# Routing on rows without norm factor and shift, in a two-layer mixture-of-experts kernel

## The chip, the cores and the metric

The kernel runs on one core of one Trainium2 chip. Its time is the device time of that core in microseconds, median of three runs. A core has five engines with an instruction stream each: TensorE (PE in the profile; PEld is its weight load), VectorE (DVE), ScalarE (ACT), GpSimd (POOL) and SyncE (SP), which issues most DMAs. ACT and POOL issue DMAs too. An engine executes in program order; semaphores order the engines among each other.

## The reference

A model of two layers on 256 latent and 256 context tokens of width 1024, float32. Each layer runs a mixer (attention in layer 0, an S5 scan with a gated linear unit, GLU, in layer 1) and then a mixture of 32 experts (MoE), two per token. Layer 1 computes latent tokens alone. Cut to what matters here:

```python
def rmsnorm(h, g):      return h * lax.rsqrt(jnp.mean(h * h, -1, keepdims=True) + 1e-6) * g
def modulate(h, shift, scale):  return h * (1.0 + scale) + shift
# per layer i; m_l = split of silu(c) @ mod_w[i] + mod_b[i] into 6 vectors
h = h + m_l[2] * mixer(modulate(rmsnorm(h, norm1_g[i]), m_l[0], m_l[1]))
t = modulate(rmsnorm(h, norm2_g[i]), m_l[3], m_l[4])      # rows of the MoE
g_logits = t @ w_group + b_group                           # 4 groups, best one taken
e_logits = t @ w_router + b_router                         # 32 experts, two best of the group
# combine[token, expert]: softmax weights of the two
y = sum_e combine[:, e] * ((silu(t @ w_gate[e]) * (t @ w_up[e])) @ w_down[e])
h = h + m_l[5] * y
```

Context tokens go the same way in layer 0 with vectors of their own. Per row, t = r · (h · scale) + shift, where r is the norm's factor (one number a row), and scale = (1 + m[4]) · g and shift = m[3] are vectors over the 1024 columns.

## The kernel before

All instructions are issued in a program order written by hand: generators yield between steps, and `along(main, others)` (L213) runs one step of each other generator after each step of the main one.

**Layer 0.** `attention` ends with the output products: `out(t)` (L439) for the tiles t = 0 to 3 (128 rows each; 0 and 1 context, 2 and 3 latent) issues 16 products (L445), one a round. Beside it run `beside` (products with `mod_w` for layer 1's vectors, L142, in half vectors of four steps, one half every four rounds; the last two halves run after tile 3) and, for each tile whose output is done, `Moe.prep` (L597) and `Moe.route` (L647), one step a round. After tile 3, `build` loads two experts' weights (`ahead(2)`, SP's queue) and runs what is left of the preparation, with the last `mod_w` steps between its steps. Weights pass through a pool of 1 MiB slots ("ring" and "more").

`prep(n, j)` of tile n with vectors j: row t = h · scale on VectorE (L609) and the sum of squares on ACT; r on POOL; then t = t · r + shift in two halves (L618, VectorE); in layer 0 a store of t to `td` in DRAM; eight transposes by TensorE (L626) copied into tT; logits by eight products with the router table `wr` (L632; 40 columns: 4 groups, 4 empty, 32 experts), plus the bias `br`. In layer 1 the rows are then split in a high and a low part (ACT L640, POOL L642), as transposed weights for the gather by products.

`route`: maxima, indices and one-hots on VectorE (`oh`, `ob` L673); products that count earlier tokens of each expert (L683), giving a position to each token; two one-hots "A" of the slot (L717) and products that place token numbers, later the weights, into 64 slots per expert (`place`, L719). The last tile's route calls `count` (the number of rounds of 64 slots, read at the end only).

In layer 0 `start()` (L770) then makes indices and issues three gathers on POOL's queue (L836, rows of `td` by index, 128 rows for a pair of experts), then expert 2's weights on the same queue; `turned` (L850) transposes a gathered pair. `experts` (L952) runs experts 0 to 31: `hidden` (L863) gate and up products, `down` (L884), `combine` (L928).

**Layer 1.** `s5.glu(1, wg)` is the GLU's last half: 32 steps n = 0 to 31, three products each (L1745), its weights split in high and low parts by VectorE and POOL (L1714). Between steps `build` runs two steps of tile 0's prep at n = 12, two of tile 1's at n = 16, and one of tile 0's at each even n from 18 on. The GLU's result for a tile leaves through VectorE and ACT (L1753 to L1758). What is left follows behind the GLU in the order of the string LAST, 0 and 1 being tiles and 2 `moe.opening`. `open()` (L780) makes the first four experts' rows by products of the high and low parts with one-hots of the slots (`take` L767); `quad` does it for later fours.

`load_rows` issues on POOL's queue the norm gain and the shift and scale rows, broadcast to 128 partitions (`mod.row`); `scale_rows` makes scale of them (L593); `tables` then loads `wr` (L555, L556), `br` and iotas. The end of layer 0's row loads, the tables and the output stage lie close together in time.

Of the kernel before, what the change touches and what calls it, by code (L numbers as in the profile page):

```python
# [244 lines left out]
def attention(c, mod, par, tail):  # L245
# [3 lines left out]
    with ExitStack() as ctx:  # L249
# [264 lines left out]
class Moe:  # L514
# [7 lines left out]
    def __init__(self, c, layer, tiles, wk, ps, lent=None):  # L522
# [18 lines left out]
        self.oh = wk.tile([128, nt, 2, 32], F32, name="oh")  # L541
# [25 lines left out]
    def more(self, wk, ps):  # L567

        self.wk2, self.ps2 = wk, ps
        self.opening, self.opened = self.open(), 0  # L570
        self.gates()
# [6 lines left out]
    def load_rows(self):  # L578
# [4 lines left out]
        for j in dict.fromkeys(j for _, j in self.tiles_j):  # L583
# [3 lines left out]
            self.rows[j] = r  # L587

# [7 lines left out]

    def prep(self, n, j):  # L597

# [17 lines left out]
        for f in range(2):  # L616
            s = slice(512 * f, 512 * f + 512)
            nc.vector.scalar_tensor_tensor(t[:, s], t[:, s], st[:, 3:4], shift[:, s], op0=OP.mult, op1=OP.add)  # L618
            yield
        if self.xg is not None:  # L620
            nc.scalar.dma_start(self.td[128 * n:128 * n + 128], t)
        tT = wk.tile([128, KT, 128], F32, name="tT", tag="t4", bufs=T4)
        for b in range(2):
            p = self.bank(("xt", "gu")[b])
            for k in range(4):
                nc.tensor.transpose(p[:, 128 * k:128 * k + 128], t[:, 512 * b + 128 * k:512 * b + 128 * k + 128], c.ident)  # L626
            c.evac(tT[:, 4 * b:4 * b + 4, :], p.rearrange("p (k n) -> p k n", k=4))
            yield
        yield
        p = self.bank("gu")  # L630
# [16 lines left out]
    def route(self, n, L):  # L647
# [49 lines left out]
        if self.one:  # L697
            yield
# [1262 lines left out]
```

## Time and profile before

| | |
|---|---|
| median of three runs | 1160.03 us (1157.13 to 1165.32) |
| the profiled execution | 1162.29 us, its span 1160.3 us |
| granted TensorE clock, mean | 0.951 of full speed |
| busy: TensorE / VectorE / ACT / POOL | 993.9 (86%) / 729.3 (63%) / 322.9 (28%) / 140.6 (12%) us |
| DMA | 331.75 MB, mean 286 GB/s |
| layer 0: output stage with tiles 0 to 2 / to the first expert | 283 to 383.42 / to 410.60 us |
| layer 1: GLU's last quarter / to the first expert / experts to the end | 829.60 to 859.90 / to 886.04 / to 1160.30 us |

Times of single instructions count from the span's start. A line of the timeline has the start, the busy time of a run of like instructions, engine, line of the code, output and input, their number and, in brackets, the idle time ahead and what ended it. In a table of windows "(x9)" is a number of instructions, "PEclk" the granted clock as a share of full speed (1.00 is 2.4 GHz, 0.50 is 1.2 GHz), and "DMA share" the mean busy share of 16 DMA engines.

### The profile page before, as it was taken

Reading aid. Unit: us, or ns where it says so; the run is one execution under the profiler, and the core shown is the slowest. Engines: PE = TensorE matmul, PEld = TensorE weight load, DVE = VectorE, ACT = ScalarE, POOL = GpSimd, SP = SyncE. Lnnn points to the kernel's source line nnn. Section 1 sums busy time; section 2 is a strip of 40 time slices with the busy share of each in tenths; the row PEclk is TensorE's granted clock in tenths of the full one; section 3 lists DMA queues with packets and bytes.
Section 4 is the critical chain, followed back from the end, with each engine's and each line's share of the span. In section 5 each row is a group of like instructions: output and inputs, shape, how many; then the busy total and the mean of one; then the engine's idle time right before and its main releaser. Section 6 shows DMA issues by size and latency. Waiting matters only on the chain. (4 is left out here: it accounts for less than half of the span.)

```text
span 1160.3 us, 17551 instructions
## 1 busy us (share of the span) xinstructions
PE 993.9 (86%) x6639; PEld 561.9 (48%) x6639; DVE 729.3 (63%) x1800; ACT 322.9 (28%) x703; POOL 140.6 (12%) x212
## 2 busy tenths in 40 slices
PE   2798889979998499999988876579868999999996
PEld 1443444544444355555544432365656555555552
DVE  7679988894325513555788987499874444444444
ACT  3332334343000123121221212793532212221110
POOL 2211121123100200000000002112321000000000
PEclk9999999989988789999998988889988999999998
DMA  9954854764993799999885854899976999999941
GB/s 297 340 158 149 285 211 156 263 210 166 385 342 126 274 415 415 400 410 349 326 340 214 330 209 153 201 210 316 397 264 267 378 384 378 376 379 380 382 168 37
DMA packets 88232, 331.75 MB, mean 286 GB/s; under 512 B 10040, under 2 KB 18968, under 8 KB 69712
## 3 DMA queue, kind: packets, MB, share of 16 engines
q1 hardware_dynamic: 68736, 290.05, 68.0%
q10 hardware_dynamic: 11424, 21.12, 5.2%
q0 software_dynamic: 7984, 19.42, 5.0%
q8 instruction: 54, 0.88, 0.3%
q14 instruction: 34, 0.28, 0.1%
HBM read 313.76 MB, written 20.99 MB: 289 GB/s over the span
## 5 line engine op out<-in xcount | busy, mean ns | idle before, releaser
L863 PE MATMUL gu<-ring,xq 128*64 128x256 f32 x1056 | 144.3, 388 | 2.7 <-DVE sl L868 2.6
L863 PE MATMUL gu<-more,xq 128*64 128x256 f32 x992 | 136.0, 386 | 0.8 <-DVE sl L868 0.8
L928 PE MATMUL co<-yh,oT 128*128 128x512 f32 x188 | 88.0, 468 | 26.6 <-DVE z L919 8.9
L863 PEld LDWEIGHTS gu<-ring,xq 128*64 128x64 f32 x1056 | 81.3, 139 | 60.2 <-issue 23.9
L863 PEld LDWEIGHTS gu<-more,xq 128*64 128x64 f32 x992 | 76.9, 138 | 54.4 <-issue 22.9
L352 PE MATMUL acc<-ring,uT 128*128 128x512 f32 x192 | 93.0, 617 | 2.9 <-ACT uT L328 2.9
L867 ACT ACTIVATE sl<-gu 64x256 f32<-64x256 f32 x64 | 24.1, 377 | 243.6 <-PE gu L863 243.6
L936 DVE TENSOR_TENSOR sum<-sum,co 128x512 f32<-128x512 f32 x92 | 59.5, 682 | 33.3 <-PE co L928 33.3
L928 PE MATMUL co<-yl,oT 128*128 128x512 f32 x188 | 78.2, 416 | 0.3 <-DVE yl L913 0.3
L876 DVE COPY hT<-ht 128x128 f32<-128x128 f32 x64 | 18.4, 287 | 87.0 <-PE ht L874 86.8
L868 DVE TENSOR_TENSOR sl<-gu,sl 64x256 f32<-64x256 f32 x64 | 27.3, 426 | 64.5 <-ACT sl L867 49.7
L884 PE MATMUL y<-ring,hT 128*64 128x512 f32 x272 | 67.2, 616 | 0.4 <-DVE hT L876 0.4
L928 PEld LDWEIGHTS co<-yh,oT 128*128 128x128 f32 x188 | 36.0, 191 | 61.7 <-DVE z L919 15.9
L884 PE MATMUL y<-more,hT 128*64 128x512 f32 x240 | 58.0, 604 | 0.4 <-DVE hT L876 0.4
L352 PEld LDWEIGHTS acc<-ring,uT 128*128 128x128 f32 x192 | 35.0, 196 | 37.3 <-issue 32.8
L142 PE MATMUL gv<-ring,cT 128*32 128x256 f32 x512 | 35.6, 421 | 18.2 <-DMA ring<-mod_w 18.2
L930 DVE TENSOR_TENSOR h<-h,co 128x512 f32<-128x512 f32 x64 | 41.1, 681 | 8.5 <-PE co L928 8.5
L928 PEld LDWEIGHTS co<-yl,oT 128*128 128x128 f32 x188 | 36.6, 195 | 7.5 <-DVE yl L913 4.4
L836 POOL DMA_INDIRECT xg<-td,row x16 | 16.1, 1006 | 196.6 <-PE xt L850 186.1
L407 ACT ACTIVATE pr<-sc,mx 128x256 f32<-128x256 f32 (+1 forms) x32 | 18.6, 580 | 74.7 <-DVE mx L406 74.6
L913 DVE SCALAR_TENSOR_TENSOR yl<-z,pt,yh 128x512 fp32r<-128x512 f32 x30 | 22.5, 751 | 25.4 <-ACT yh L912 25.4
L912 ACT ACTIVATE yh<-z,pt 128x512 fp32r<-128x512 f32 x30 | 21.6, 722 | 55.9 <-DVE z L919 55.9
(430 smaller groups left out, 1868.4 us busy)
## 6 DMA issues: line engine op xcount, KB each, us to landing
ring<-moe_w_down SPq DMA_DIRECT2D x34, 1024.0 KB, 10.2
ring<-moe_w_gate SPq DMA_DIRECT2D x33, 1024.0 KB, 11.1
ring<-moe_w_up SPq DMA_DIRECT2D x33, 1024.0 KB, 8.9
ring<-mod_w SPq DMA_DIRECT2D x32, 1024.0 KB, 8.2
more<-moe_w_gate SPq DMA_DIRECT2D x30, 1024.0 KB, 6.4
more<-moe_w_up SPq DMA_DIRECT2D x30, 1024.0 KB, 8.8
more<-moe_w_down SPq DMA_DIRECT2D x29, 1024.0 KB, 11.2
more<-mod_w SPq DMA_DIRECT2D x16, 1024.0 KB, 7.1
```

What stands on the lines that cost most here:

```text
L142: nc.tensor.matmul(self.bank[i, b][32 * q:32 * q + 32, o:o + 256], self.cT[:, k, :], self.tiles[i, ch, k // 2][:, k % 2, 256 * q:256 * q + ...
L352: nc.tensor.matmul(acc, uT[:, k, 128 * t:128 * t + 128], wq[b][k // 4][:, k % 4, :], start=(k == 0), stop=(k == KT - 1))
L407: nc.scalar.activation(pr[:, 0:nk], s[:, 0:nk], AF.Exp, bias=mx[:, h, 0:1], accum_out=mx[:, h, 1:2])
L863: nc.tensor.matmul(p[s:s + 64, 0:HID], xT[k], w[k // 4][:, k % 4, :], start=(k == 0), stop=(k == KT - 1), skip_group_check=True)
L867: nc.scalar.activation(sl, p[0:64, 0:HID], AF.Silu)
L868: nc.vector.tensor_tensor(sl, p[64:128, 0:HID], sl, op=OP.mult)
L884: self.c.nc.tensor.matmul(p[o:o + 64, :], hT[:, f, :], wd[f][:, 512 * n:512 * n + 512], start=(f == 0), stop=(f == 1), skip_group_check=True)
L912: nc.scalar.activation(hi, y, AF.Copy, scale=w)
L913: nc.vector.scalar_tensor_tensor(lo, y, w, hi.bitcast(F32), op0=OP.mult, op1=OP.subtract)
L928: nc.tensor.matmul(p, oh[:, 128 * n:128 * n + 128], y, start=(i == 0), stop=(i + 1 == len(rows)))
L930: nc.vector.tensor_tensor(h, h, p, op=OP.add)
L936: nc.vector.tensor_tensor(a, a, p, op=OP.add)
```

## The change

The router's transposes and products take rows h · scale alone. The logits become r · product + `lb`, where `lb` (made once for each j by `base`, in steps of its own ahead of the first tile of that j) is shift times the table, plus the bias: a product on VectorE of the table with the shift as a column, a sum, and one TensorE product with ones over the partitions. `load_rows` loads the shift as columns of [128, 8], in pieces of four bytes, on POOL's queue: `sr` in both layers, `se` in layer 1.

Layer 0: t · r + shift is still made, behind the transposes, and stored. `wait(one, more)` puts more rounds between the steps of prep and route (`more` where the tiles have two sorts of vectors, as in layer 0; `one` in layer 1). `soon` runs the first four steps of tile 3's prep in rounds 11 to 14 of its own output. Only expert 0's weights are loaded ahead; those of 1, 2 and 3 on POOL's queue between and behind the gathers. `count` moves to expert 1; the last four `mod_w` steps stand behind the logits.

Layer 1: the high part is h · scale · r by ACT, the low part on VectorE; the shift is added to gathered rows where they leave PSUM (`moved` on ACT, an addition on VectorE). The dictionary EARLY says at which GLU step which generator takes a step (0 and 1: prep of tiles 0 and 1; 2: the opening). The route of tile 0 and its placement lie inside the GLU with it.

```diff
...
@@ -498,10 +498,22 @@
         b = beside()
         rest = [b]
+        preps = [moe.prep(t, 1 if t < 2 else 0) for t in range(4)]
+        def soon(g):
...
+            for _ in range(10):
+                yield
+            for _ in range(4):
+                next(g)
+                yield
         for t in range(4):
+            if t == 3:
+                rest.append(soon(preps[3]))
             along(out(t), rest)
-            rest.append(moe.prep(t, 1 if t < 2 else 0))
-        return [x for x in rest if x is not b], halves
+            rest.append(preps[t])
+        return [x for x in rest if x in preps], halves
...
+        self.columns = {"(k p) -> p k": wk.tile([128, KT, 2], F32, name="sr")}
+        if not lent:
+            self.columns["(p k) -> p k"] = wk.tile([128, KT, 2], F32, name="se")
...
+        self.lb = {}
+        self.opening = self.open()
...
+            for name, x in self.columns.items():
+                c.nc.gpsimd.dma_start(x[:, :, j], c.mv[self.layer, j, 3 * D:4 * D].rearrange(name, k=KT))
...
             self.scaled.add(j)
         return r
+    def base(self, j):
+        nc, wk = self.c.nc, self.wk
+        x = self.row_tile("lbx")[:, 0:40 * KT].rearrange("p (k n) -> p k n", k=KT)
+        ones = wk.tile([128, 128], F32, name="A", tag="A", bufs=4 if self.one else 2)
+        nc.vector.memset(ones, 1.0)
+        shift = self.columns["(k p) -> p k"][:, :, j:j + 1]
+        nc.vector.tensor_tensor(x, self.wr[:, :, 0:40], shift.to_broadcast([128, KT, 40]), op=OP.mult)
+        y = wk.tile([128, 40], F32, name="L", tag="L", bufs=2)
+        nc.vector.tensor_reduce(y, x.rearrange("p k n -> p n k"), axis=AX.X, op=OP.add)
+        yield
+        yield from self.wait(0, 2)
+        p = self.bank("gu")
+        nc.tensor.matmul(p[:, 0:40], ones, y, start=True, stop=True)
+        self.lb[j] = wk.tile([128, 40], F32, name=f"lb{j}")
+        nc.vector.tensor_add(self.lb[j], p[:, 0:40], self.br)
...
         t = self.row_tile("t")
         st = wk.tile([128, 4], F32, name="st", tag="st", bufs=2)
         yield
+        if j not in self.lb:
+            yield from self.base(j)
+        tT = wk.tile([128, KT, 128], F32, name="tT", tag="t4", bufs=T4)
         for f in range(2):
             s = slice(512 * f, 512 * f + 512)
+            nc.vector.tensor_mul(t[:, s], h[:, s], scale[:, s])
             sq = wk.tile([128, 512], BF, name="sq", tag="sq")
             nc.scalar.activation(sq, h[:, s], AF.Square, accum_out=st[:, f:f + 1])
-            nc.vector.tensor_mul(t[:, s], h[:, s], scale[:, s])
-            if f == 0:
-                yield
-        nc.vector.tensor_add(st[:, 2:3], st[:, 0:1], st[:, 1:2])
-        rstd(c, st[:, 3:4], st[:, 2:3], D)
-        yield
-        yield
-        for f in range(2):
-            s = slice(512 * f, 512 * f + 512)
-            nc.vector.scalar_tensor_tensor(t[:, s], t[:, s], st[:, 3:4], shift[:, s], op0=OP.mult, op1=OP.add)
-            yield
-        if self.xg is not None:
+            if f:
+                nc.vector.tensor_add(st[:, 2:3], st[:, 0:1], st[:, 1:2])
+                rstd(c, st[:, 3:4], st[:, 2:3], D)
+            yield
+            yield from self.wait(0, 1)
+            p = self.bank("xt")
+            for k in range(4):
+                nc.tensor.transpose(p[:, 128 * k:128 * k + 128], t[:, 512 * f + 128 * k:512 * f + 128 * k + 128], c.ident)
+            x, p = tT[:, 4 * f:4 * f + 4, :], p.rearrange("p (k n) -> p k n", k=4)
+            if f:
+                nc.vector.tensor_copy(x, p)
+            else:
+                nc.scalar.activation(x, p, AF.Copy)
+                yield
+        r = st[:, 3:4]
+        if self.xg is None:
...
+            x = t.rearrange("p (q k) -> p k q", k=KT)
+            hi, lo = (y.rearrange("p (k q) -> p k q", k=KT) for y in (hi, lo))
+            ks = [slice(0, 4), slice(4, 8)]
+            for k in ks:
+                nc.scalar.activation(hi[:, k], x[:, k], AF.Copy, scale=r)
+            def low(k):
+                nc.vector.scalar_tensor_tensor(lo[:, k], x[:, k], r, hi[:, k].bitcast(F32), op0=OP.mult, op1=OP.subtract)
+            low(ks[0])
+            self.low = lambda: low(ks[1])
+            if n + 1 < self.nt:
+                self.low()
+            self.parts.append((hi, lo))
+        else:
+            for f in range(2):
+                s = slice(512 * f, 512 * f + 512)
+                nc.vector.scalar_tensor_tensor(t[:, s], t[:, s], r, shift[:, s], op0=OP.mult, op1=OP.add)
             nc.scalar.dma_start(self.td[128 * n:128 * n + 128], t)
-        tT = wk.tile([128, KT, 128], F32, name="tT", tag="t4", bufs=T4)
-        for b in range(2):
-            p = self.bank(("xt", "gu")[b])
-            for k in range(4):
-                nc.tensor.transpose(p[:, 128 * k:128 * k + 128], t[:, 512 * b + 128 * k:512 * b + 128 * k + 128], c.ident)
-            c.evac(tT[:, 4 * b:4 * b + 4, :], p.rearrange("p (k n) -> p k n", k=4))
-            yield
-        yield
+            if n + 1 < self.nt:
+                yield
         p = self.bank("gu")
         for k in range(KT):
             nc.tensor.matmul(p[:, 0:40], tT[:, k, :], self.wr[:, k, 0:40], start=(k == 0), stop=(k == KT - 1))
         L = wk.tile([128, 40], F32, name="L", tag="L", bufs=2)
-        nc.vector.tensor_add(L, p[:, 0:40], self.br)
-        if self.xg is None:
-            hi, lo = self.part.get(n) or self.part_tiles(n)
-            x = t.rearrange("p (q k) -> p k q", k=KT)
-            hi, lo = (y.rearrange("p (k q) -> p k q", k=KT) for y in (hi, lo))
-            nc.scalar.activation(hi, x, AF.Copy)
-            for k in range(0, KT, 2):
-                nc.gpsimd.tensor_tensor(lo[:, k:k + 2], x[:, k:k + 2], hi[:, k:k + 2].bitcast(F32), op=OP.subtract)
-            self.parts.append((hi, lo))
+        nc.vector.scalar_tensor_tensor(L, p[:, 0:40], r, self.lb[j], op0=OP.mult, op1=OP.add)
         yield
         yield from self.route(n, L)
...
-        yield
-        yield
+        yield from self.wait(2, 4)
         p = self.bank("gu")[:, 0:32]
...
-            for _ in range(self.nt - self.opened):
-                next(self.opening)
+            next(self.opening)
         V.tensor_reduce(self.pe[:, n], x, axis=AX.X, op=OP.add)
         rhs = self.rhs[:, n]
         for k in range(2):
...
-        hots = self.place(n, self.pe[:, n], [rhs[:, k, 0:32] for k in range(2)], slice(0, 32))
+        hots = self.hots(self.pe[:, n])
+        yield from self.wait(0, 3)
+        self.place(n, hots, [rhs[:, k, 0:32] for k in range(2)], slice(0, 32))
         if self.xg is not None and n + 1 == self.nt:
             self.start()
...
-            yield
+        yield from self.wait(1, 0)
...
-        self.place(n, self.pe[:, n], [rhs[:, k, 32:64] for k in range(2)], slice(32, 64), hots)
-    def place(self, n, pe, rhs, s, hots=None):
-        nc, V = self.c.nc, self.c.nc.vector
+        yield from self.wait(0, 3)
+        self.place(n, hots, [rhs[:, k, 32:64] for k in range(2)], slice(32, 64))
+    def wait(self, one, more):
+        for _ in range(one if self.one else more):
+            yield
+    def hots(self, pe):
+        out = [self.wk.tile([128, 128], F32, name="A", tag="A", bufs=4 if self.one else 2) for k in range(2)]
+        for k in range(2):
+            self.c.nc.vector.tensor_scalar(out[k], self.slot, pe[:, k:k + 1], None, op0=OP.is_equal)
+        return out
+    def place(self, n, hots, rhs, s):
...
+            self.c.nc.tensor.matmul(self.acc[:, s], hots[k], rhs[k], start=(n + k == 0 and s.start == 0),
+                                    stop=(n == self.nt - 1 and k == 1), skip_group_check=True)
...
-        q = self.bank("xt")
+        q = self.bank("co")
...
         cnt, full = wk.tile([128, 1], F32, name="cnt"), wk.tile([128, MAXR], F32, name="full")
@@ -770,38 +826,55 @@
     def start(self):
         self.indices()
-        for k in range(3):
-            self.gather(k)
         c = self.c
         c.queue = c.nc.gpsimd
-        self.first[2] = self.weights(2)
+        self.gather(0)
+        self.gather(1)
+        self.first[1] = self.weights(1)
+        self.gather(2)
+        for e in (2, 3):
+            self.first[e] = self.weights(e)
         c.queue = c.nc.sync
...
+    def shifts(self):
+        return self.columns["(p k) -> p k"][:, :, self.one[0]]
     def open(self):
         if self.xg is not None:
-            for n in range(self.nt):
-                if n + 1 == self.nt:
-                    self.count()
-                self.opened += 1
-                yield
+            yield
             return
         g = self.onehot_tile("t4")
-        p = [self.bank(b) for b in ("y0", "y1", "co", "co")]
         for n in range(self.nt):
             self.onehots(g, n, 0)
             if n + 1 == self.nt:
-                self.count()
-            for k in range(KT):
-                self.take(p[k // 2][:, 256 * (k % 2):256 * (k % 2) + 256], k, n, g[:, n], k % 2 == 0)
-            self.opened += 1
+                self.low()
+            else:
+                yield
+            if n == 0:
+                p = [self.bank(b) for b in ("y0", "y1", "co", "co")]
+            for i, x in enumerate(self.parts[n]):
+                for k in range(KT):
+                    self.c.nc.tensor.matmul(p[k // 2][:, 256 * (k % 2):256 * (k % 2) + 256], x[:, k, :], g[:, n],
+                                            start=(n + i + k % 2 == 0), stop=(n + 1 == self.nt and i == 1), skip_group_check=True)
             yield
         self.xq = []
+        sh = self.shifts()
         for s in range(2):
             x = self.row_tile("xq").rearrange("p (k n) -> p k n", k=4)
             for i in range(2):
-                self.c.evac(x[:, 2 * i:2 * i + 2], p[2 * s + i].rearrange("p (k n) -> p k n", k=2))
+                y, k = p[2 * s + i].rearrange("p (k n) -> p k n", k=2), 4 * s + 2 * i
+                if i:
+                    self.c.nc.vector.tensor_tensor(x[:, 2:4], y, sh[:, k:k + 2, None].to_broadcast([128, 2, 256]), op=OP.add)
+                else:
+                    self.moved(x[:, 0:2], y, k)
             self.xq.append(x)
+    def moved(self, out, p, k):
+        for i in range(2):
+            self.c.nc.scalar.activation(out[:, i], p[:, i], AF.Identity, bias=self.shifts()[:, k + i:k + i + 1])
...
-            nc.scalar.activation(out[-1][:, 2 * (s % 2):2 * (s % 2) + 2], p.rearrange("p (k n) -> p k n", k=2), AF.Copy)
+            self.moved(out[-1][:, 2 * (s % 2):2 * (s % 2) + 2], p.rearrange("p (k n) -> p k n", k=2), 2 * s)
...
-LAST = "1001111100112"
+EARLY = {4: 0, 8: 0, 10: 0, 12: 0, 13: 1, 14: 1, 17: 0, 18: 1, 20: 0, 25: 0, 26: 0, 28: 0, 30: 0, 31: 2}
...
-            beside = chain(*(mod.steps(1, ch, range(4 * h, 4 * h + 4)) for ch, h in halves), range(4), (next(moe.opening) for _ in range(3)))
+            moe.ahead(1)
+            beside = chain(*(mod.steps(1, ch, range(4 * h, 4 * h + 4)) for ch, h in halves))
...
-                    if n in (12, 16):
-                        for _ in range(2):
-                            next(prep[n // 16])
-                    if n >= 18 and n % 2 == 0:
-                        next(prep[0])
+                    if n in EARLY:
+                        next((*prep, moe.opening)[EARLY[n]], None)
...
-                if n == 2:
-                    next(moe.opening)
-                else:
-                    next(prep[n], None)
-            for _ in chain(*prep, moe.opening):
+            for n in map(int, "121111"):
+                next((*prep, moe.opening)[n])
+            for _ in chain(moe.opening, *prep):
                 pass
```

Left out: the same edits in `overflow` (a loop for experts with over 64 tokens) and some names.

## Rows read from the trace of the kernel before

**Rows 1.** Busy time by stage; columns in the first line

```profile
core 0: us, PE busy (x) PEld busy (x) DVE busy (x) ACT busy (x) POOL busy (x), PEclk, DMA share, GB/s
...
388.00:437.20 49.20, 34.28 (x228) 21.09 (x230) 13.15 (x54) 11.05 (x23) 10.22 (x16) 0.79 1.02 410
829.60:859.90 30.30, 24.36 (x108) 18.69 (x108) 24.85 (x33) 8.35 (x14) 10.22 (x12) 1.00 0.76 270
859.90:886.04 26.14, 15.59 (x92) 14.59 (x91) 18.25 (x76) 10.30 (x19) 7.75 (x11) 0.67 0.92 369
886.04:1160.30 274.26, 259.14 (x1696) 143.68 (x1696) 120.27 (x241) 50.85 (x91) 1.05 (x4) 0.99 0.80 311
```

**Rows 2.** The same view, around three stalls of layer 0's output stage

```profile
316.67:321.75 5.08, 1.68 (x9) 1.40 (x9) 3.74 (x23) 1.49 (x7) 0.36 (x1) 0.91 1.03 407
...
321.75:328.37 6.62, 6.62 (x38) 2.43 (x38) 0.00 (x0) 0.00 (x0) 1.69 (x3) 0.55 0.74 290
...
349.45:354.53 5.08, 2.13 (x11) 1.80 (x9) 3.73 (x23) 1.49 (x7) 0.36 (x1) 0.71 0.80 325
...
354.53:360.13 5.60, 5.60 (x38) 2.08 (x38) 0.00 (x0) 0.00 (x0) 0.00 (x0) 0.66 0.00 0
...
377.14:380.60 3.46, 1.28 (x11) 0.99 (x9) 2.66 (x17) 1.49 (x7) 0.00 (x0) 1.00 0.00 0
```

**Rows 3.** Timeline of layer 0, columns in the first line

```profile
start us, us, engine line op out<-in xcount [idle before <-releaser]
...
301.08 3.70 PE L445 MATMUL acc<-ring,oT 128*128 128x512 f32 x8
...
380.60 2.82 PE L445 MATMUL acc<-ring,oT 128*128 128x512 f32 x6
...
387.91 0.66 PE L626 MATMUL xt<-ident,t 128*128 128x128 f32 x4 [0.90 <-DVE t L618]
...
390.58 1.98 PE L632 MATMUL gu<-wr,tT 128*128 128x40 f32 x16 [0.69 <-ACT tT L98]
...
394.97 0.19 DVE L673 TENSOR_TENSOR ob<-oh 128x32 bf16<-128x32 f32 x1
...
399.56 1.15 POOL L836 DMA_INDIRECT xg<-td,row  x1 [9.38 <-DVE sc L700]
...
407.75 1.11 PE L850 MATMUL xt<-ident,xg 128*128 128x128 f32 x4 [5.69 <-DMA xg<-td,row]
...
410.60 4.83 PE L863 MATMUL gu<-ring,xq 128*64 128x256 f32 x32
```

**Rows 4.** POOL's timeline; issues (KB each, us to landing) at 286.35 and 284.1

```profile
286.35 0.90 POOL L556 DMA_DIRECT2D wr<-moe_w_router  x1
...
wr<-moe_w_router POOLq DMA_DIRECT2D x1, 128.0 KB, 18.8
...
r<-mv POOLq DMA_DIRECT2D x2, 512.0 KB, 18.2
```

**Rows 5.** Timeline of the GLU, TensorE and VectorE

```profile
839.30 0.50 PE L1745 MATMUL o<-wl,z0z 128*128 128x512 f32 x1 [1.11 <-POOL wl L1714]
...
841.04 2.35 DVE L1714 TENSOR_TENSOR wl<-ring,wh 128x1024 fp32r<-128x1024 f32 x2
...
843.32 0.68 DVE L1753 TENSOR_TENSOR g<-o,bg 128x512 f32<-128x512 f32 x1
...
846.15 0.69 DVE L1758 TENSOR_TENSOR h<-h,g 128x512 f32<-128x512 f32 x1
...
846.75 1.22 DVE L593 SCALAR_TENSOR_TENSOR r<-r,g 128x1024 f32<-128x1024 f32 x1
```

**Rows 6.** Timeline behind the GLU, up to the first expert

```profile
861.30 0.69 DVE L609 TENSOR_TENSOR t<-h,r 128x512 f32<-128x512 f32 x1
...
880.66 0.19 DVE L673 TENSOR_TENSOR ob<-oh 128x32 bf16<-128x32 f32 x1
...
886.04 3.67 PE L863 MATMUL gu<-ring,xq 128*64 128x256 f32 x32
```

More of the change, by code (lines that the diff above doesn't have):

```diff
@@ L540, in __init__ @@
         self.tok = wk.tile([128, nt], F32, name="tok")
-        self.oh = wk.tile([128, nt, 2, 32], F32, name="oh")
+        self.oh = wk.tile([128, nt, 2, 32], F32, name="oh", tag="oh")
         self.rhs = wk.tile([128, nt, 2, 64], F32, name="rhs")
@@ L569, in more @@
         self.wk2, self.ps2 = wk, ps
-        self.opening, self.opened = self.open(), 0
         self.gates()
@@ L706, in route @@
             V.tensor_scalar(rhs[:, k, 32:64], oh[:, k], m[:, k:k + 1], None, op0=OP.mult)
-        self.place(n, self.pe[:, n], [rhs[:, k, 32:64] for k in range(2)], slice(32, 64), hots)
-    def place(self, n, pe, rhs, s, hots=None):
-        nc, V = self.c.nc, self.c.nc.vector
+        yield from self.wait(0, 3)
[9 more added lines that the diff above has]
+    def place(self, n, hots, rhs, s):
         if n == 0 and s.start == 0:
             self.acc = self.bank("ht")
-        if hots is None:
-            hots = [self.wk.tile([128, 128], F32, name="A", tag="A", bufs=4 if self.one else 2) for k in range(2)]
-            for k in range(2):
-                V.tensor_scalar(hots[k], self.slot, pe[:, k:k + 1], None, op0=OP.is_equal)
         for k in range(2):
-            nc.tensor.matmul(self.acc[:, s], hots[k], rhs[k], start=(n + k == 0 and s.start == 0),
-                             stop=(n == self.nt - 1 and k == 1), skip_group_check=True)
-        return hots
+            self.c.nc.tensor.matmul(self.acc[:, s], hots[k], rhs[k], start=(n + k == 0 and s.start == 0),
+                                    stop=(n == self.nt - 1 and k == 1), skip_group_check=True)
     def slots(self, name=""):
@@ L1014, in experts @@
                         pieces = (self.combine(n, j, f, parts, k) for k in [e // 2 - 1] for f in range(2) for n, j in tiles)
+            if e == 1:
+                self.count()
             if e > 14:
@@ L1033, in overflow @@
         n = nc.values_load(self.rounds[0:1, 0:1], min_val=1, max_val=MAXR)
-        pe, pos = wk.tile([128, self.nt, 2], F32, name="pe_r"), wk.tile([128, self.nt, 32], F32, name="pos_r")
+        pe = wk.tile([128, self.nt, 2], F32, name="pe_r")
+        pos = self.wk.tile([128, self.nt, 2, 32], F32, name="pos_r", tag="oh")[:, :, 0]
         V.tensor_copy(pe, self.pe)
@@ L1040, in overflow @@
             for t in range(self.nt):
-                self.place(t, pe[:, t], [self.rhs[:, t, k] for k in range(2)], slice(0, 64))
+                self.place(t, self.hots(pe[:, t]), [self.rhs[:, t, k] for k in range(2)], slice(0, 64))
             ts = self.slots("o")
@@ L1073, in overflow @@
                             self.take(p[:, W * k:W * k + W], k, t, g[:, t], k == 0)
-                V.tensor_copy(xT, p.rearrange("p (k n) -> p k n", k=KT))
+                p = p.rearrange("p (k n) -> p k n", k=KT)
+                if self.xg is not None:
+                    V.tensor_copy(xT, p)
+                else:
+                    V.tensor_tensor(xT, p, self.shifts()[:, :, None].to_broadcast([128, KT, W]), op=OP.add)
                 for _ in self.hidden([xT[:, k, :] for k in range(KT)], wg, wu):
```

4 lines of the change are left out of this document (1 added, 3 removed).

## Prediction

> **What bounds the kernel now.** I read the busy time by stage first, then the slices of single stalls, then the order of time around the two places that the change touches. In both expert stages TensorE sets the pace: 259.14 busy of 274.26 us in layer 1 [rows 1]. A later or earlier first expert of layer 1 (886.04) therefore moves the end one to one. In layer 0 the first four experts take 410.60 to 437.20, and there the DMA engines are full too (share 1.02, 410 GB/s) [rows 1, 3]: an early start pays only if the weights come.
>
> Ahead of layer 0's experts TensorE runs the attention's output products with the preparation and routing of tiles 0 to 2 mixed in. Three times it stands in a route, in order behind one-hots and weights that VectorE has yet to make: idle 5.08 - 1.68 = 3.40, 5.08 - 2.13 = 2.95 and 3.46 - 1.28 = 2.18 us. After two of these the granted clock is 0.55 and 0.66 of full speed for 6.62 and 5.60 us, that is the 1.2 GHz level for most of it: 2.98 and 1.90 us lost [rows 2]. Sum 13.4 us.
>
> From the last product of tile 3 (380.60 + 2.82 = 383.42, called X) it is 16.1 us to the first gather, 24.3 to its first transpose, which waited for the DMA, and 27.2 to the first expert [rows 3].
>
> In layer 1 the GLU's last quarter takes 30.3 us with TensorE busy 24.36; from its end to the first expert pass 26.14 us with TensorE busy 15.59 at clock 0.67 [rows 1]. VectorE is the late engine inside the GLU: TensorE's product at 839.30 is the 11th step's (n=10), while VectorE finishes the weight split at 843.39 and the first half's activation chain only from 843.32 to 846.84 [rows 5].
>
> **Layer 0, the output stage.** The new waits (four steps between route and counting, three before each placement) put several output products between VectorE's work and TensorE's need of it. A round of one product is 3.70 / 4 = 0.93 us [rows 3]; five rounds cover the 2.6 us from the logits' end (392.56) to the one-hots' (395.16) [rows 3]. So the 13.4 us go.
> A new wait comes: the first tile's `base` multiplies the router table by the shift column. Its matmul stands after round 5 of tile 1's products: 301.08 + 2 x 0.93 = 302.9 [rows 3]. Behind it, in order, are all products of the stage. The router table is issued at 286.35 and lands 18.8 us later, at 305.15 [rows 4]. Two column loads of 1024 four-byte pieces are put ahead of it on POOL's queue. No row shows such a load. The nearest, the two table loads with 1024 pieces each, together landed 305.15 - 302.3 = 2.9 us behind the last row load [rows 4]. So the two column loads cost between 0 and 2.9 us; I take 1.5, since they carry fewer bytes than the tables: table at 306.6. The product of 320 and the sum to 40 elements are not in the trace; as VectorE operations of less than 512 elements they cost between nothing and 2 x 0.69 [rows 6]; I take 1.0: 307.6. Stall 307.6 - 302.9 = 4.7 (2.2 to 6.5), and the slow clock after it, between nothing and 2.98 [rows 2]; I take 2.3, as the idle time is as long as the first route's. The second `base` (tile 2) finds its table landed. Net: 13.4 - 4.7 - 2.3 - 0.3 for the extra matmuls = 6.1 us earlier (3.6 to 10.9).
> The Trainium skill speaks against these loads: by its page DMA: Bandwidth & Descriptors, section Specifications, transfers below 512 bytes are not at line rate. Its section Anatomy of one DMA fits about 2.0 us fixed per load from this queue, so as an estimate two loads one after the other cost 4.0, and the sum would be 6.1 - 2.5 = 3.6; the rows' value is 1.5, and no run here shows a four-byte load yet.
>
> **Layer 0, start of the experts.** Tile 3's first half is squared, scaled and transposed beside its own second half, and transposes no longer wait for the norm's factor: they come 387.91 - 383.42 = 4.5 us after X now [rows 3], and after three VectorE operations of 0.69 then, about 2 us sooner. The count's operations leave for expert 1. Against that, tile 2's held-back routing now lies here: 2.66 us of VectorE work [rows 2], and the last four `mod_w` steps stand behind the logits. These cancel within 1 us: gather at X' + 15.5 instead of + 16.1. The gather now has at most two weight loads ahead instead of six, but its own latency stays; 8.2 us before [rows 3], I take 6.4 (4 to 8.2). First expert at X' + 25 instead of + 27.2.
> Then supply: the up weights of expert 0 need a slot that those last `mod_w` steps free, at about X' + 11. From there up to expert 4's gate and up weights the queues carry 15 MiB (two loads of expert 0, nine of experts 1 to 3, two of expert 4, four gathers of 0.5), 15.7 MB, at 410 GB/s [rows 1] 38.4 us: X' + 49 to 51. TensorE asks for them at X' + 25 + 26.6 = 51.6, before at X + 53.8. So the gain here is 1.5 us (from -2, if the new order makes expert 3 wait and this isn't caught up, to +3). POOL waits with expert 3's last load for expert 0's gate slot; the pair copies and the fourth gather queue behind it, not needed before the third and seventh expert. Layer 0 in sum: 7.6 us earlier (2 to 13).
>
> **Layer 1, inside the GLU.** Program order on VectorE: weight split (ends 843.39), now the row scaling (1.22, moved up from 846.75), then the chain 843.32 to 846.84 (3.5 us), then `base` (1.0 and a fill, 1.2): 843.39 + 1.22 + 3.5 + 1.2 = 849.3 [rows 5]. TensorE passes n=10 at 839.8 [rows 5] and now meets the base matmul there: 9.5 us idle with 21 of 32 GLU steps behind it. Before, it waited only for the split, to about 842. A step is three matmuls of 24.36 / 108 = 0.226 [rows 1], 0.68 us. From 849.3: 21 steps 14.3; three sets of transposes 3 x 0.66 and the logits 1.98 [rows 3]; placement and counting about 1.2: 868.8 at the least. To that come the slow clock after the idle, 3.0 (0 to 3.0, as after the first route [rows 2]); the copy ahead of the logits, 0.8; the route: activation chain 3.5 and route about 2.4 against five steps of 3.4, 2.5; and the one-hots ahead of the placement, 1.4. GLU end 876.5, against 859.9.
> After it: the chain to the scaling 861.30 - 859.90 = 1.4 and 0.69 [rows 6], transposes 0.66, copy 0.7, logits 1.98, 2.6 to the one-hots [rows 3], then before 880.85 to 886.04 = 5.2 to the first expert [rows 6], less the count: 4.5. Sum 12.5 instead of 26.14. First expert at 889.0 against 886.04: 3.0 later. Without slow clock and waits it is 881.3, 4.7 earlier; with twice the waits and a slow clock in the gathering matmuls (half of 2 us again) some 7 later.
> No price: the low parts move from POOL to VectorE, two operations each the size of the two scale-and-shift operations that tile loses, so VectorE's sum stands; if it did not, 1.5 us per tile. The shift added at the slot copies is hidden by products of the running expert; without that cover it would be one more ACT start per copy. The count at expert 1 is hidden the same way.
>
> **Sum.** -7.6 + 3.0 = -4.6, with about 0.5 for the count's tiny matmuls and split copies -4.1. The profiled execution's span of 1160.3 becomes 1156.2; its own time was 1162.29, the median of the three runs 1160.03. From the median: 1156.
>
> **Rivals.** (1) It does in layer 1 what it is for: GLU end near its least, first expert 881, and the table in layer 0 costs 2.5 only with no clock loss: -(10.6 + 3) - 4.7 = -18, 1142. For it: 11 us of idle TensorE behind the GLU are there to win [rows 1]. Against: VectorE's order above. Chance 0.17.
> (2) The other side: the four-byte column loads hold POOL's queue, and the table, `base` and the whole output stage wait. It decides from the table's landing: at 311 the forecast's gain is gone, from 322 on the kernel is 1% slower. With 8 us for each load: +12, 1172. Against: the table loads have as many pieces and took 2.9 together [rows 4]. Chance 0.10.
> (3) Layer 0's gain is given back because weights 1 to 3 are ordered after the routing, with DMA at 1.02 already [rows 1]: 1160 + 3, 1163. Chance 0.13.
>
> **How the numbers follow.** The forecast's case has 0.60 and its own range 1149 to 1163, from the bounds above. The range 1143 to 1168 takes in (3), nearly all of (1), and leaves out (2) and the forecast's far ends, about 0.15. About 1% (11.6 us) is what a measurement of this kernel tells from no change. Faster by more: (1) and 0.03 of the forecast, 0.20. Slower: (2) and 0.02, 0.12. Same 0.68.
>
> **What the profile would show.** Right: no slow clock around the routes of tiles 0 to 2; one gap of TensorE of some 5 us before the first base matmul; in the GLU a gap of 7 to 10 us ahead of the 12th step, ended by VectorE; 12 to 13 us from GLU end to the first expert. Wrong: that gap under 3 us (then rival 1), a router table landing after 311 (rival 2), expert 2 or 3 of layer 0 waiting for DMA over 5 us (rival 3).

## The result and the profile after

The changed kernel takes 1174.87 us, median of four runs (1171.68 to 1175.54), against 1159.39 for the kernel before in the same runs: ratio 1.012, 95% interval 1.0078 to 1.0162. It is slower, by 1.2%; the forecast was 1156, its range 1143 to 1168. The execution profiled below took 1171.68 us, span 1169.7. It is the fastest of the four, so the two profiles differ by 9.4 us where the medians differ by 15.5.

Busy time by stage, after (columns as in [rows 1]): layer 0 from the last output product to the first expert and on to the down product of expert 2; then the GLU's last quarter, what follows up to layer 1's first expert, and the experts.

```profile
376.89:399.78 22.89, 14.37 (x117) 9.93 (x113) 13.66 (x60) 2.20 (x8) 9.69 (x14) 0.70 0.81 281
399.78:437.49 37.71, 31.27 (x179) 16.67 (x179) 5.09 (x14) 8.08 (x14) 4.99 (x11) 0.82 1.02 417
835.04:878.69 43.65, 31.33 (x138) 25.58 (x136) 28.92 (x61) 12.85 (x22) 10.34 (x12) 0.84 0.54 197
878.69:895.28 16.59, 10.27 (x64) 9.46 (x62) 12.01 (x41) 6.86 (x14) 1.14 (x2) 0.77 1.00 390
895.28:1169.70 274.42, 258.85 (x1699) 143.54 (x1698) 120.58 (x244) 57.25 (x118) 1.21 (x5) 0.99 0.81 315
```

The same view of the kernel before, for three of these stages between the same events:

```profile
410.60:435.88 25.28, 24.96 (x176) 14.35 (x175) 4.26 (x10) 7.96 (x14) 2.44 (x4) 0.95 1.02 414
...
829.67:859.65 29.98, 24.04 (x105) 18.41 (x104) 24.73 (x32) 8.35 (x14) 10.22 (x12) 1.00 0.76 268
859.65:886.04 26.39, 15.84 (x94) 14.83 (x92) 18.30 (x76) 10.30 (x19) 7.75 (x11) 0.68 0.92 369
```

In layer 0 the first expert starts at 399.78 instead of 410.60, 10.8 us earlier; at the down product of expert 2 (437.49 against 435.88) the kernel is 1.6 us behind. The 12.4 us were lost in between: 6.1 more idle on TensorE and 6.3 more busy, most of it from a lower clock (0.82 against 0.95). In layer 1 the GLU takes 13.7 us more and what follows 9.8 less. Between these two places the changed kernel takes 397.6 us and the one before 393.8, the longest and the shortest of all twelve profiles there; no cause of these 3.8 us is shown.

Timeline of layer 0, after:

```profile
286.18 0.90 POOL L573 DMA_DIRECT2D wr<-moe_w_group  x1 [0.29 <-POOL wr L572]
...
290.90 0.88 POOL L574 DMA_DIRECT2D wr<-moe_w_router  x1 [3.82 <-DMA g<-norm_g]
...
307.29 0.49 DVE L623 TENSOR_TENSOR lbx<-wr,sr 128x320 f32<-128x320 f32 x1 [8.92 <-DMA wr<-moe_w_router]
...
308.63 0.65 PE L629 MATMUL gu<-L,A 128*128 128x40 f32 x2 [6.65 <-DVE L L625]
...
375.01 1.88 PE L445 MATMUL acc<-ring,oT 128*128 128x512 f32 x4
...
392.45 1.16 POOL L909 DMA_INDIRECT xg<-td,row  x1 [1.69 <-DVE sc L749]
...
396.95 1.09 PE L923 MATMUL xt<-ident,xg 128*128 128x128 f32 x4 [1.99 <-DMA xg<-td,row]
...
399.96 0.58 POOL L89 DMA_DIRECT2D more<-moe_w_gate  x1
...
404.50 0.55 POOL L89 DMA_DIRECT2D more<-moe_w_up  x1 [3.96 <-issue]
...
405.08 0.33 SPq L89 DMA_DIRECT2D ring<-moe_w_gate  x1
...
415.41 2.52 PE L936 MATMUL gu<-more,xq 128*64 128x256 f32 x14 [2.06 <-DMA more<-moe_w_up]
...
424.44 0.62 PE L936 MATMUL gu<-more,xq 128*64 128x256 f32 x2 [0.86 <-DMA more<-moe_w_gate]
...
428.25 3.67 PE L936 MATMUL gu<-more,xq 128*64 128x256 f32 x14 [3.19 <-DMA more<-moe_w_up]
```

The loads issued at 399.96 and 404.50 (gate and up of expert 3, POOL's queue) and at 405.08 (gate of expert 4, SP's queue), with us from issue to landing:

```profile
more<-moe_w_gate POOLq DMA_DIRECT2D x1, 1024.0 KB, 24.3
...
more<-moe_w_up POOLq DMA_DIRECT2D x1, 1024.0 KB, 23.7
...
ring<-moe_w_gate SPq DMA_DIRECT2D x1, 1024.0 KB, 9.0
```

Expert 4's gate, issued 5 us later, landed at 414.1; expert 3's at 424.3, with loads of experts 1 and 2 still ahead of it on its own queue, and its up weights at 428.2, for which TensorE waited. Expert 2's up weights were waited for too (415.41).

Timeline of the GLU's last quarter, after:

```profile
836.23 0.69 DVE L1841 TENSOR_TENSOR h<-h,g 128x512 f32<-128x512 f32 x1
836.38 5.62 POOL L1794 TENSOR_TENSOR wl<-ring,wh 128x1024 fp32r<-128x1024 f32 x2 [14.14 <-ACT wh L1793]
...
837.56 2.19 DVE L1841 TENSOR_TENSOR h<-h,g 128x512 f32<-128x512 f32 x1
839.67 4.55 DVE L1794 TENSOR_TENSOR wl<-ring,wh 128x1024 fp32r<-128x1024 f32 x2
...
842.32 0.39 PE L1825 MATMUL o<-wl,z0z 128*128 128x512 f32 x1
...
844.14 1.21 DVE L612 SCALAR_TENSOR_TENSOR r<-r,g 128x1024 f32<-128x1024 f32 x1
...
848.10 0.69 DVE L1838 TENSOR_TENSOR h<-h,g 128x512 f32<-128x512 f32 x1
...
849.96 0.49 DVE L623 TENSOR_TENSOR lbx<-wr,sr 128x320 f32<-128x320 f32 x1 [1.02 <-DMA wr<-moe_w_router]
...
851.40 0.62 PE L629 MATMUL gu<-L,A 128*128 128x40 f32 x2 [8.69 <-DVE L L625]
```

TensorE has passed n = 10 at 842.7 and stands for 8.69 us at `base`, while VectorE does the weight split, the row scaling and the first tile's chain; the table costs 1.02 of it. VectorE's order is that of [rows 5], with the row scaling moved up and `base` added.

### The profile page after: what moved, and what is told of

Its sections match the earlier page's. It is cut to its first block, busy times and chain, and to the rows that moved or that the text cites. A ratio compares the mean times of both kernels' runs of the same rounds, so it can differ in the third digit from the quotient of the medians.

```text
span 1169.7 us, 17609 instructions
## 1 busy us (share of the span) xinstructions
PE 1005.0 (86%) x6645; PEld 567.7 (49%) x6645; DVE 734.3 (63%) x1812; ACT 330.7 (28%) x735; POOL 141.5 (12%) x214
## 5 line engine op out<-in xcount | busy, mean ns | idle before, releaser
L936 PE MATMUL gu<-more,xq 128*64 128x256 f32 x992 | 140.0, 391 | 6.1 <-DMA more<-moe_w_up 5.3
L957 PE MATMUL y<-ring,hT 128*64 128x512 f32 x272 | 69.8, 636 | 0.4 <-DVE hT L949 0.4
L1639 ACT ACTIVATE un<-ut,cols 128x32 f32<-128x32 f32 x128 | 35.3, 412 | 6.3 <-PE ut L1632 6.3
```

The source lines that it names most:

```text
L936: nc.tensor.matmul(p[s:s + 64, 0:HID], xT[k], w[k // 4][:, k % 4, :], start=(k == 0), stop=(k == KT - 1), skip_group_check=True)
L957: self.c.nc.tensor.matmul(p[o:o + 64, :], hT[:, f, :], wd[f][:, 512 * n:512 * n + 512], start=(f == 0), stop=(f == 1), skip_group_check=True)
L1639: nc.scalar.activation(u4[:, k, s], ut[:, 64 * k + 32 * s:64 * k + 32 * s + 32], AF.Identity, bias=shift, scale=scale)
```

## Experiments

**Each layer alone.** e1 has the changed layer 0 and the old layer 1, e2 the reverse (the old class as `MoeOld`, with its GLU order and LAST, or with the old end of the attention and the old `ahead(2)` loop, put back whole).

```diff
-                moe = Moe(c, 1, ((2, 0), (3, 0)), *pools(right, "moe1", "right"))
+                moe = MoeOld(c, 1, ((2, 0), (3, 0)), *pools(right, "moe1", "right"))
```

and for e2

```diff
-            first = lambda lent: Moe(c, 0,
+            first = lambda lent: MoeOld(c, 0,
```

> Layer 0 as changed, layer 1 as in the kernel before (its rows, parts, GLU order and string LAST). Theory: layer 0 loses, since the first expert comes some 11 us earlier but experts 2 and 3 wait for weights whose loads were issued behind the gathers: first expert at about 400, behind the kernel before by 1.5 to 3 us from expert 4 on, and GLU end to first expert of layer 1 again 26 us. Time 1160 to 1168, 2 to 6 us above before. Rival: all the loss is in layer 1; then this is at or under before, 1150 to 1159.

> Layer 1 as changed, layer 0 and the end of the attention as in the kernel before. Theory: the base product stops TensorE at the 12th step of the GLU for 8 to 9 us, the tail behind the GLU is 16 to 17 us instead of 26, sum 4 us above before: 1162 to 1165. Rival: layer 1 costs nothing and layer 0 has it all, 1157 to 1160.

e1: 1.0007 of before (0.9973 to 1.0041). e2: 1.0107 (1.0073 to 1.0141). So layer 0 came out even, and layer 1 alone costs some 12 us. Against before both expectations missed (e1's time, 1161.82, lies in its range, 1160 to 1168): layer 0's loss is smaller and layer 1's three times what the stages above show. Windows of e1, GLU quarter, tail, experts:

```profile
834.83:860.43 25.60, 23.33 (x108) 18.82 (x106) 21.02 (x26) 7.83 (x13) 10.35 (x12) 1.00 0.72 268
860.43:887.90 27.47, 17.53 (x94) 16.70 (x93) 18.85 (x76) 9.55 (x19) 7.76 (x11) 0.57 0.87 352
887.90:1158.90 271.00, 255.84 (x1697) 142.20 (x1696) 119.72 (x240) 51.63 (x91) 1.04 (x4) 1.00 0.81 314
```

The same of e2, and then three slices of its experts:

```profile
836.65:880.97 44.32, 31.41 (x138) 25.60 (x136) 30.37 (x63) 12.97 (x22) 9.96 (x12) 0.81 0.60 231
880.97:897.13 16.16, 9.65 (x63) 8.88 (x61) 12.01 (x41) 6.86 (x14) 1.13 (x2) 0.79 0.97 369
897.13:1173.40 276.27, 260.67 (x1699) 144.30 (x1698) 120.54 (x244) 57.24 (x118) 1.20 (x5) 0.98 0.81 313
...
897.13:901.13 4.00, 4.00 (x23) 2.37 (x24) 0.97 (x4) 0.00 (x0) 1.20 (x5) 0.60 0.78 322
1149.00:1153.00 4.00, 3.85 (x19) 2.02 (x19) 2.73 (x5) 0.72 (x1) 0.00 (x0) 0.69 0.00 0
1163.10:1167.10 4.00, 3.84 (x6) 1.56 (x7) 1.37 (x2) 0.00 (x0) 0.00 (x0) 0.63 0.18 43
```

GLU and tail: 53.1 in e1, 60.5 in e2 (56.4 and 60.2 in before and after). The experts: 271.0 and 276.3, with TensorE idle 15.2 and 15.6: nearly the same waits at another clock. The first slice is the slow clock of the tail reaching into the first expert; the later two dips are in the profile of before too, and not in e1's.

Two pairs of runs differ in layer 1 alone: e1 and the changed kernel, and e5 and e3 below. From layer 0's expert 2 (its down product) to the end the new layer 1 takes 11.6 and 12.2 us more in their profiles: 7.2 and 8.5 in GLU and tail, 3.4 and 4.9 in the experts. The stages above show less because GLU and tail of before's profile (56.4) are long: the three others with the old layer 1 (e1, e5, e9) take 51.7 to 53.1. In its GLU quarter TensorE is idle for 5.9 us, in e1's for 2.3. The comparison of e2's profile with before's says less: of its 13.1 us, 6.0 lie ahead of that down product in layer 0, whose code is the same.

**Layer 0: the order of the weight loads.** e3 is the changed kernel with the old loads (`ahead(2)`, three gathers, then `weights(2)`); e5 the same with the old layer 1; e10 keeps the loads behind the routing, but on one queue. e3:

```diff
-            moe.ahead(1)
+            moe.ahead(2)
...
         c.queue = c.nc.gpsimd
-        self.gather(0)
-        self.gather(1)
-        self.first[1] = self.weights(1)
-        self.gather(2)
-        for e in (2, 3):
-            self.first[e] = self.weights(e)
+        for k in range(3):
+            self.gather(k)
+        self.first[2] = self.weights(2)
         c.queue = c.nc.sync
```

and e10, against the changed kernel, in `start`

```diff
-        c.queue = c.nc.gpsimd
-        self.gather(0)
...
-        c.queue = c.nc.sync
+        for k in range(3):
+            self.gather(k)
+        c.nc.sync.dma_start(c.dp.tile([128, 16], U32, name="hold"), self.row)
+        for e in (1, 2, 3):
+            self.first[e] = self.weights(e)
```

> The changed kernel, but weights as before: experts 0 and 1 ahead on SP's queue, then three gathers, then expert 2 on POOL's queue. Theory of the order: the waits of experts 2 and 3 for weights (6.1 us, and the slow clock with them) go, the gather takes about 8 us again instead of 4.5; 5 to 8 us under the changed kernel, 1166 to 1170. Rival of the bandwidth: the DMA engines are full either way, the first expert comes 6 us later or the waits stay, and the time is within 2 us of the changed kernel.

> Layer 0 as changed but with the loads of the kernel before (experts 0 and 1 ahead, expert 2 behind the gathers), layer 1 as in the kernel before. Theory: the changed routing of layer 0 is worth 10 to 14 us and the order of the weight loads takes all of it back; with the old order and the old layer 1 nothing takes it back: 0.987 to 0.992 of before, the end of layer 0 some 8 us earlier. Rival: the DMA engines bound the first experts, 0.996 to 1.000 of before.

> The changed kernel with the weights of experts 1 to 3 on SP's queue, where those of expert 4 and later are, held back until the indices exist by a small load of them ahead (so no earlier than on POOL's queue). Theory of overtaking: on two queues the loads of experts 4 and 5 share the DMA engines with those of 2 and 3, which are needed first (gate of expert 4 landed 10 us ahead of gate of expert 3); on one queue they come in order, and TensorE's waits for weights, 6.1 us, fall under 2.5: 4 to 8 us under the changed kernel. Rival of the late start: the loads begin only behind the routing, and the waits stay at 5 to 8 us, the time within 3 us.

e3: 1.0005 (0.9976 to 1.0034), 13 us under the changed kernel, where 5 to 8 were expected. e5: 0.9922 (0.9894 to 0.9951), at the upper edge of what was expected. e10: 0.9999 (0.9965 to 1.0033), 14 us under it, where 4 to 8 were expected. In e10 SP issues the held loads at 398.00, no earlier than the routing allows, and the only wait of TensorE for a DMA between the last output product and expert 4 is the gather's:

```profile
380.82 1.88 PE L445 MATMUL acc<-ring,oT 128*128 128x512 f32 x4
...
398.00 0.33 SPq L832 DMA_DIRECT2D hold<-row  x1
...
407.32 1.09 PE L920 MATMUL xt<-ident,xg 128*128 128x128 f32 x4 [6.54 <-DMA xg<-td,row]
...
435.64 1.94 PE L954 MATMUL y<-more,hT 128*64 128x512 f32 x8
```

The gather takes longer again (6.54 of waiting against 1.99) and the waits for weights are gone. The loads begin behind the routing here too, so the rival of the late start, by which the waits stay, is out. The rest is not quite equal: counted from the end of the last output product (called X' in the prediction), the loads of experts 1 to 3 start at 15.7 us in e10 and at 18.1 in the changed kernel, and the first expert at 27.5 and 22.9. But expert 3's up weights land at 42.0 instead of 51.3, and a start 2.4 us earlier does not make that. e10 also moves the third gather ahead of expert 1's loads; that was not tried alone.

From X' to the down product of expert 2 pass 60.6 us in the changed kernel, 52.7 in e3 and 52.9 in e10, and 61.8 in e1 against 53.9 in e5. So some 8 us of the 10 to 14 that the times show lie there; where the rest lies the profiles do not tell.

**Layer 0: the late table.** e8 loads the two columns in 128 pieces of 32 bytes (other layout, same number of loads); e9 is e5 with `tables()` called ahead of `load_rows()`. e8, and then e9:

```diff
-        self.columns = {"(k p) -> p k": wk.tile([128, KT, 2], F32, name="sr")}
+        self.columns = {"(k p) -> p k": wk.tile([128, 2, KT], F32, name="sr").rearrange("p j k -> p k j")}
...
-                c.nc.gpsimd.dma_start(x[:, :, j], c.mv[self.layer, j, 3 * D:4 * D].rearrange(name, k=KT))
+                c.nc.gpsimd.dma_start(x[:, :, j], c.mv[self.layer, j, 3 * D:4 * D].rearrange(name if self.one else "(p k) -> p k", k=KT))
```

```diff
         if lent:
+            self.tables()
             c.nc.gpsimd.memset(self.xg, 0.0)
         self.load_rows()
...
-                box[0].tables()
```

> The changed kernel with layer 0's two column loads in 128 pieces of 32 bytes instead of 1024 of 4 bytes, same count of loads; the columns then hold the shift in another order, so layer 0's routing is not the reference's. Theory: the router table is issued at 290.9 instead of 286.4 because it is two more loads down POOL's queue and has to wait for the first one's landing, not because of the pieces: the table is still issued at 290 to 291.5 and lands at 306 to 308, TensorE's stop at base stays 6 to 7 us. Rival of the four-byte pieces: issue at 286 to 288, landing at 304 to 305, a stop of 3 us or less.

> Layer 0 as changed with the old order of weight loads, layer 1 as before, and in layer 0 the router tables loaded ahead of the row and column loads. Theory: TensorE's stop at the first base (6.65 us, then slow clock) waits for the router table alone, which goes out late; issued first it lands near 300, the stop is under 2 us, the last output product comes 5 to 8 us earlier, and the time is 4 to 8 us under the same kernel with the tables behind the rows (which was 0.992 of before): 0.985 to 0.989 of before. Rival: what is won there is given back in the wait for the first weights or in the rows that now land later: 0.991 to 0.994.

e8 (one run, 1175.21), POOL's timeline:

```profile
286.77 0.91 POOL L573 DMA_DIRECT2D wr<-moe_w_group  x1 [0.29 <-POOL wr L572]
291.18 0.89 POOL L574 DMA_DIRECT2D wr<-moe_w_router  x1 [3.49 <-DMA g<-norm_g]
```

The table waits all the same for the landing of the first of the eight loads ahead of it (gain, rows and columns of two sorts, group table) and lands 15.8 us after its issue, at 307.0; the stop was 5.0 us, less than expected, the products ahead of it having run later. The count makes most of the delay: the table is issued 8.95 us behind the first of these loads in e8, 10.05 in the changed kernel and 4.44 in the kernel before, so at most 1.1 us can be the pieces'. The kernel before has the same wait at the ninth load of its own series, the router's bias:

```profile
290.93 0.55 POOL L559 DMA_DIRECT2D br<-moe_b_router  x1 [2.69 <-DMA g<-norm_g]
```

e9: 0.9857 (0.9814 to 0.9899), 1146.34 us: faster than both kernels and, by the ratios, 0.65% (7.5 us) under e5, as expected. Its timeline shows no stop at `base`:

```profile
280.69 0.89 POOL L575 DMA_DIRECT2D wr<-moe_w_router  x1
...
301.57 1.98 PE L445 MATMUL acc<-ring,oT 128*128 128x512 f32 x4
303.39 0.31 PE L630 MATMUL gu<-L,A 128*128 128x40 f32 x2
```

**Layer 1: the stop in the GLU.** e4 puts `base` behind the transposes, ahead of the logits. Its result differs from the reference's; its instructions are the same, in another order. e6 moves tile 0's steps. e4, and then e6:

```diff
-        if j not in self.lb:
-            yield from self.base(j)
         tT = wk.tile([128, KT, 128], F32, name="tT", tag="t4", bufs=T4)
...
+        if j not in self.lb:
+            yield from self.base(j)
         p = self.bank("gu")
         for k in range(KT):
```

```diff
-EARLY = {4: 0, 8: 0, 10: 0, 12: 0, 13: 1, 14: 1, 17: 0, 18: 1, 20: 0, 25: 0, 26: 0, 28: 0, 30: 0, 31: 2}
+EARLY = {4: 0, 8: 0, 21: 0, 22: 1, 23: 0, 24: 1, 25: 0, 26: 1, 27: 0, 30: 0, 31: 0}
-            for n in map(int, "121111"):
+            for n in map(int, "002121111"):
-                next((*prep, moe.opening)[n])
+                next((*prep, moe.opening)[n], None)
```

e7 is e6 with e3's loads.

> The changed kernel with base's steps behind the tile's transposes, right ahead of its logits, in both layers; sums and loads are the same. Theory: TensorE's stops at base (6.65 us in layer 0, 8.69 in layer 1) come from where base stands, ahead of products that need none of it; with it late they go, and the slow clock after them: 10 to 18 us under the changed kernel, 1157 to 1165. Rival: the table's landing sets the logits anyway and the stops move there, within 4 us of the changed kernel.

> The changed kernel, but in the GLU tile 0's first work for TensorE (the base product) stands at step n = 21 instead of 10, the rest of it up to the one-hots in steps 23 to 31, the placement behind the GLU. Theory: TensorE stops at n = 10 because it meets tile 0 before VectorE, still busy with the weight split and the first tile's chain, can have anything of it ready, whichever product of tile 0 stands there (base late only moved the stop to the transposes); with the steps at 21 and later the stop is under 3 us, the GLU 30 to 34 us long instead of 43.7, the tail 19 to 23 instead of 16.6: 5 to 10 us under the changed kernel. Rival: the router table's late landing or the clock sets it, and the stop moves along: within 3 us of the changed kernel.

> The changed kernel with both edits: the old order of the weight loads in layer 0 and the GLU steps at 21 and later. If the two causes are separate, their gains add up: 12 and 5 to 10 us under the changed kernel, 0.988 to 0.996 of before. If one hides the other, about as with the weight loads alone, 1.000 of before.

e4: 1.0041 (1.0011 to 1.0071), 9 us under the changed kernel, but not for the reason expected in layer 1; there the stop stayed, now at tile 0's transposes:

```profile
845.54 1.09 PE L655 MATMUL xt<-ident,t 128*128 128x128 f32 x4 [8.64 <-DVE t L645]
```

So both products of tile 0 that were tried there, `base` and the transposes, wait for VectorE. What e4's profile wins is layer 0's (the last output product ends at 372.3 instead of 376.9). e6: 1.0031 (1.0008 to 1.0054), 10 us under the changed kernel; `base` and the windows of its GLU and tail:

```profile
850.79 0.39 PE L629 MATMUL gu<-L,A 128*128 128x40 f32 x2 [0.46 <-DVE L L625]
```

```profile
833.11:868.43 35.32, 31.29 (x128) 24.31 (x126) 27.36 (x48) 13.28 (x23) 10.20 (x12) 0.86 0.74 282
868.43:891.18 22.75, 14.11 (x72) 13.42 (x71) 14.65 (x57) 6.94 (x14) 1.14 (x2) 0.65 0.85 333
```

The stop is gone, the sum is 58.1, between before's and after's (54.4 in e7's profile, with the same layer 1). e7: 0.9979 (0.9943 to 1.0014), less gain than expected and above e5, which has the old layer 1. So layer 1's edit, with its steps late, still costs some 0.6% (the two intervals just overlap) and wins nothing here. Nor do the gains add up: the late steps are worth 0.9% with the changed loads (e6), and with the old ones 0.3% (e7 against e3), which is not clear of noise.

## Why the prediction was wrong

**Layer 0's output stage: right, by another cause.** X came at 375.01 + 1.88 = 376.89, 6.5 earlier (forecast 6.1), of which 1.1 are that the stage began earlier. That the 13.4 us of the old waits go is borne out by e9, which has no stop: its stage, from the first of these output products to X', takes 71.8 us against 86.9 before. The table landed at 290.90 + 16.3 = 307.2 (forecast 306.6), the stop was 6.65 (4.7 forecast, 6.5 its bound). But the forecast laid the delay to the time the column loads take on the queue; the trace and e8 show a wait for a landing eight loads back. That the landing comes out within 0.6 us is luck: the issue was 4.6 later, and issue to landing took 16.3 instead of 18.8. The lower sum (3.6) by the Trainium skill's page DMA: Bandwidth & Descriptors, section Anatomy of one DMA, finds no support in an X 6.5 earlier. Of the limit of 512 bytes in its section Specifications no run here shows anything: pieces of 4 and of 32 bytes, which do nearly alike, are both below it.

**Start of the experts: right.** Gather at X' + 15.6 (15.5), first expert at X' + 22.9 (25).

**Supply: the step that failed in layer 0.** The sum took the queues as one line of 15.7 MB and asked only whether expert 4's weights came by X' + 51.6. They came at X' + 37 for its gate, ahead of expert 3's (X' + 51.3 for its up weights). For start and supply together it had a gain of 1.5 (2.2 from the earlier first expert, less 0.7); from X' to the down product of expert 2 the trace has a loss of 8.1 (60.6 us against 52.5 before): 4.3 gained up to the first expert, 12.4 lost behind it. Rival 3 had the place, the sign, its mark (waits over 5 us: 6.1, experts 2 and 3 together) and, by e1's +0.8, its price for layer 0, and the forecast gave it 0.13.
Of queues that share the engines, the Trainium skill's page DMA: Bandwidth & Descriptors, section Queues, rings and completion order, says that each DMA engine takes turns between the queues that have work for it. The trace agrees: expert 4's gate, issued 5.1 us behind expert 3's, landed 10.2 ahead of it, and e10 without the second queue has no such wait.

**Layer 1: the mechanism right, the size off.** Stop 8.69 (9.5 forecast), GLU 13.7 longer (forecast 16.6), tail 16.6 (12.5, with a slow clock only in its bound; the granted clock of the tail was 0.77), first expert 3.9 later counted from the GLU's start (3.0). By e2 the edit costs 12 us and the forecast's bound was +7. Two terms were mis-sized. The first is what the new GLU and tail were held against: the forecast took the old ones from before's profile, and in the pairs that differ in layer 1 alone the edit costs 7.2 and 8.5 there. The second is the clock: a slow one inside the longer GLU was counted, none in the experts behind it, where the same pairs lose 3.4 and 4.9 at nearly equal idle time. How much of that belongs to the edit stays open. The experts took 271.0 to 274.3 in the four profiles with the old layer 1 and 274.4 to 276.9 in the eight with the new, but late dips of the clock show in two of the four as well.

**The range.** Both misses lie on the same side: layer 0 at +0.8 (e1) instead of -7.6, layer 1 at +12.4 (e2) instead of +3.0; 1159.4 + 0.8 + 12.4 = 1172.6. The cases were priced one at a time, and none held a supply loss together with a layer 1 above its bound.

## What to carry to other kernels

Loads that are needed in order belong on one queue: on a second one they shared the engines here with loads that are needed later. A step moved under other work must not meet its engine before its inputs can exist; look at what the engine that feeds it still has in line, and count a stop's slow clock also in the stage behind it. Before adding small loads ahead of one that something waits for, count the loads in flight on that queue, and look for a wait like that of the ninth load, which the profile of the kernel before already showed here. A profile is one execution: where a stage of it is the measure for a forecast, see how far that stage differs between profiles of the same code.

## What the runs showed of the hardware

The clock: the same code for layer 1's experts took 274.26 us at a granted clock of 0.99 in before's profile [rows 1] and 271.00 at 1.00 in e1's, with TensorE idle for 15.1 and 15.2 us. With the new layer 1, e2's took 276.27 at 0.98 with 15.6 idle, and stretches of 4 us at 0.60 to 0.69, that is near the 1.2 GHz level.

VectorE beside POOL: the addition at 837.56 took 2.19 us, the same line at 836.23 0.69, and the two splits from 839.67 took 4.55 instead of 2.35 [rows 5], while POOL's own split ran from 836.38 for 5.6 us. The Trainium skill's page GPSIMD Engine Reference, section Specifications, says that the two share their way to SBUF, with contention for VectorE operations with two SBUF inputs; these rows agree, as does the operation between the two additions, at 836.84, which has one input in PSUM and took 0.68. It is not new with the change: in the kernel before, POOL's split from 833.80 on stretched two additions in its place,

```profile
834.25 2.76 DVE L1758 TENSOR_TENSOR h<-h,g 128x512 f32<-128x512 f32 x1
...
837.65 2.15 DVE L1761 TENSOR_TENSOR h<-h,g 128x512 f32<-128x512 f32 x1
```

which is 3.5 us more on VectorE there and 3.7 in the changed kernel.
